# Batched float32 A·Bᵀ on one core: fourteen of sixteen stores move to GpSimd's DMA queue and start after the eighth load

## The chip, the cores and the metric

The kernel runs on one core of one Trainium2 chip. The metric is the device time in microseconds (us) of one execution. The kernel before took 127.14 us in the median of nine runs (126.47 to 127.92). The profile is one further execution, which took 126.65 us.

## The reference

```python
batch, m, k, n = 16, 512, 512, 512
a = np.random.randn(batch, m, k).astype(np.float32)
b = np.random.randn(batch, n, k).astype(np.float32)
out = np.matmul(a, b.transpose(0, 2, 1)).astype(np.float32)
```

There are sixteen independent 512x512x512 products. Both operands have the contraction dimension k last, so both have to be transposed before TensorE can multiply them. The inputs are 2 x 16.8 MB, the output is 16.8 MB, and each byte crosses once: 33.55 MB read and 16.78 MB written.

## The kernel before, in words

**Units.** Two batch elements form a pair, and there are eight pairs. A load fetches one operand of one pair: 2 MB, each of the 128 partitions taking 16 KB that are contiguous in memory. Loads are numbered 0 to 15; even ones are `a`, odd ones are `b`. The first two are issued as two halves of 1 MB each. A store writes one batch element: 1 MB, 8 KB per partition. Stores are numbered 0 to 15, and output k is what store k writes. `ld` has seven load slots and `ob` has seven output slots.

**Compute.** VectorE casts a load to bf16 in four instructions (lines 167 to 175), into the left and right halves of k. TensorE transposes 128x128 blocks against an identity (line 247) into PSUM tile `tp`. ScalarE copies A's transposes to `ta` (line 206), VectorE copies B's to `tb` (line 187). TensorE multiplies (line 266) into `ps`, and ScalarE copies `ps` to `ob` (line 224). Each of these engines runs a loop over the pairs and is held by semaphores alone.

**Semaphores that matter here.** `s_go` tells VectorE that half a load is there (two counts for a load). `s_cd` counts the first cast of each load; a load into a used slot waits for it. `s_out` counts finished outputs; a store waits for it. `s_of` counts free output slots; ScalarE takes counts from it before it writes outputs. It starts at seven.

**Order of the DMA work.** The string `ORDER`, written by hand, holds 16 letters L (load) and 15 letters S (store). SyncE (SP in the profile) walks it in the first loop (lines 92 to 118): for an L it waits for `s_cd` where the slot was used, then issues the load; for an S it waits for `s_out`, then issues the store. Since SP is one instruction stream, a letter waits for all letters before it. The DMA engines work through what SP issues in that order. The string begins with seven loads, has four more loads between the first two S, and ends with nine S.

GpSimd (POOL in the profile) walks the same string in the second loop (lines 123 to 145). For an L it waits until the load has landed and passes that on as `s_go`. For an S it waits until an old store has landed and passes that on as `s_of`. Store 0 alone is issued by GpSimd (line 135), after the fourth load has landed and output 0 is finished. ScalarE takes two counts of `s_of` at the head of each pair.

At the end SP waits for the last seven stores (lines 119, 120 and 279).

Of the kernel before, what the change touches and what calls it, by code (L numbers as in the profile page):

```python
# [10 lines left out]
def kernel(  # L11
# [6 lines left out]
    nc = tc.nc  # L18
    P = 128
    batch, M, K = a.shape  # L20
    _, N, _ = b.shape
    J = M // P
# [3 lines left out]
    pairs = batch // 2  # L26
    f32 = mybir.dt.float32
    bf16 = mybir.dt.bfloat16
    NL = 7
    NO = 7  # L30


    ORDER = "LLLLLLLSLLLLSLSSLSLSLLSSSSSSSSS"

    def sbuf(name, shape, dtype):
        return ctx.enter_context(nc.sbuf_tensor(name, shape, dtype))

    def sem(name):
        return tc.alloc_semaphore(name)

    with tc.tile_critical(no_gpsimd_drain=True):  # L41
        ident = sbuf("ident", [P, P], bf16)
        one = sbuf("one", [P, 1], f32)
        ld = sbuf("ld", [P, NL, 2 * J, K], f32)
# [5 lines left out]
        ob = sbuf("ob", [P, NO, J, N], f32)  # L50
# [3 lines left out]
        s_set = sem("s_set")  # L54
        s_ld = [sem(f"s_ld{i}") for i in range(NL)]
        s_second = [sem(f"s_second{i}") for i in range(2)]
        s_first = sem("s_first")
        s_st = [sem(f"s_st{i}") for i in range(NO)]

        def landed(n):  # L60
            return 16 * (n // NO + (n % NO > 0))


        s_go = sem("s_go")
        s_of = sem("s_of")
        s_cd = sem("s_cd")
# [11 lines left out]
        s_out = sem("s_out")  # L78
# [5 lines left out]
            out=ident[:], in_=ident[:], compare_op=mybir.AluOpType.not_equal, fill=1.0,  # L84
# [4 lines left out]

        n_ld, n_st = 0, 1
        for what in ORDER:
            if what == "L":
                u, slot = n_ld // 2, n_ld % NL
                src = (a if n_ld % 2 == 0 else b)[2 * u:2 * u + 2].rearrange(
                    "e (p j) k -> (e p) j k", j=2 * J
                )
                if n_ld >= NL:

                    nc.sync.wait_ge(s_cd, n_ld - NL + 2)
                if n_ld < 2:
                    nc.sync.dma_start(
                        ld[:, slot, :J, :], src[:, :J, :]
                    ).then_inc(s_ld[slot], 16)
                    nc.sync.dma_start(
                        ld[:, slot, J:, :], src[:, J:, :]
                    ).then_inc(s_second[slot], 16)
                else:
                    nc.sync.dma_start(ld[:, slot], src).then_inc(s_ld[slot], 16)  # L110
                n_ld += 1
            else:
                slot = n_st % NO
                nc.sync.wait_ge(s_out, n_st + 1)
                nc.sync.dma_start(
                    out[n_st].rearrange("(p j) n -> p j n", j=J), ob[:, slot]
                ).then_inc(s_st[slot], 16)
                n_st += 1
        for n in range(batch - NO, batch - 1):
            nc.sync.wait_ge(s_st[n % NO], landed(n))  # L120


        n_ld, n_st = 0, 1
        for what in ORDER:
            if what == "L":
                got = nc.gpsimd.wait_ge(s_ld[n_ld % NL], 16 * (n_ld // NL + 1))
                if n_ld < 2:
                    got.then_inc(s_go, 1)
                    nc.gpsimd.wait_ge(s_second[n_ld], 16).then_inc(s_go, 1)
                else:  # L130
                    got.then_inc(s_go, 2)
                n_ld += 1
                if n_ld == 4:
                    nc.gpsimd.wait_ge(s_out, 1)
                    nc.gpsimd.dma_start(  # L135
                        out[0].rearrange("(p j) n -> p j n", j=J), ob[:, 0]
                    ).then_inc(s_first, 16)
                elif n_ld == NL:
                    nc.gpsimd.wait_ge(s_first, 16).then_inc(s_of, 1)
            else:  # L140
                if n_st < batch - NO:
                    nc.gpsimd.wait_ge(
                        s_st[n_st % NO], landed(n_st)
                    ).then_inc(s_of, 1)
                n_st += 1

        def taker(engine):
            return lambda s, n: engine.wait_ge(s, n).then_inc(s, -n)  # L148
# [5 lines left out]
        take = taker(nc.vector)  # L154
# [3 lines left out]
        with nc.Fori(0, pairs, engines=[dve]) as u:  # L158
            for x, (h, w, s_c, s_w) in enumerate(
                ((ha, wa, s_ca, s_wa), (hb, wb, s_cb, s_wb))  # L160
            ):
                src = ld[:, bass.ds((u * 2 + x) % NL, 1)].rearrange("p o j k -> p (o j) k")
                take(s_go, 1)
                if x == 0:
# [3 lines left out]
                    out=h[:, :J, :], in_=src[:, :J, :HK]  # L168
# [4 lines left out]
                    out=h[:, J:, :], in_=src[:, J:, :HK]  # L173
                ).then_inc(s_c, 1)
                nc.vector.tensor_copy(  # L175
                    out=w[:, J:, :], in_=src[:, J:, HK:]
                ).then_inc(s_w, 1)
            for ko in range(KO):
# [5 lines left out]
                if ko == 1:  # L184
# [3 lines left out]
                    out=tb[:, ko, :],  # L188
# [5 lines left out]
        take = taker(nc.scalar)  # L194
# [3 lines left out]
        with nc.Fori(0, pairs, engines=[act]) as u:  # L198
            for ko in range(KO):

                if ko < KO - 1:
                    nc.scalar.wait_ge(s_ta, ko + 1)
                else:
                    take(s_ta, KO)
                for e in range(2):
                    c = nc.scalar.copy(  # L206
                        out=ta[:, ko, e * J * P:(e + 1) * J * P].rearrange(
                            "k (j p h) -> k j p h", j=J, h=2
                        ),
                        in_=tp[:, ko % 2, :, e * HP:(e + 1) * HP].rearrange(  # L210
                            "k (h j) p -> k j p h", h=2
                        ),
                    )
                c.then_inc(s_ea, 1)
            take(s_of, 2)
            for e in range(2):
                dst = ob[:, bass.ds((u * 2 + e) % NO, 1)].rearrange("m o j n -> m (o j) n")
                for j in range(J):
                    if j < J - 1:
                        nc.scalar.wait_ge(s_mm, j + 1)  # L220
                    else:
                        take(s_mm, J)

                    c = nc.scalar.copy(  # L224
                        out=dst[:, j, :].rearrange("m (p j) -> m p j", j=2 * J),
                        in_=ps[:, j, :].rearrange("m (j p) -> m p j", j=2 * J),
                    )
                    if e == 0:
                        c.then_inc(s_pv, 1)
                    elif j in (0, J - 1):  # L230

                        c.then_inc(s_out, 1)
# [3 lines left out]
        take = taker(nc.tensor)  # L236
# [40 lines left out]


    with tc.tile_critical(no_gpsimd_drain=True):
        nc.sync.wait_ge(s_st[(batch - 1) % NO], landed(batch - 1))  # L280


# [28 lines left out]
```

## Time and profile before

| what | value |
|---|---|
| median of nine runs | 127.14 us |
| range of the nine | 126.47 to 127.92 us |
| profiled execution | 126.65 us |
| its span, first to last instruction | 124.8 us |
| TensorE matmul busy | 93.2 us (75%) |
| VectorE busy | 70.5 us (56%) |
| ScalarE busy | 68.3 us (55%) |
| GpSimd busy | 1.4 us (1%) |
| bytes moved | 50.33 MB, mean 403 GB/s over the span |
| packet time, SP's queue q1 | 94.2% of sixteen engines' span |
| packet time, GpSimd's queue q0 | 2.0% |

The profiled execution is 1.85 us longer than its span (126.65 less 124.8) and 0.49 us shorter than the median. In the page's second part the span is cut into 40 slices of 3.12 us each: a digit is the busy share in tenths, the DMA row is the mean over the core's sixteen DMA engines, and the last row is what they moved in GB/s. The third part has a line for each DMA queue. In a line of waits or of a timeline, SPq, DVEq and PEq are the instruction sequencers of SyncE, VectorE and TensorE, and L115 is line 115 of the kernel.

The trace also has a record for each DMA packet, with queue, start, duration and size. A packet carries one partition's row: 16 KB for a load of 2 MB, 8 KB for a store or a half load. It does not say which of the sixteen DMA engines carried it. Times taken from these records are counted from the start of the span, as all others.

### The profile page before, as it was taken

The numbers are of one execution on the slowest core, as the hardware profiler recorded it, in microseconds if no ns is written. First come the engines' busy times: TensorE is split into PE (matmuls) and PEld (weight loads), VectorE is DVE, ScalarE is ACT, GpSimd is POOL, SyncE is SP. The second block draws the span as 40 slices with busy tenths as digits, with TensorE's granted clock in tenths as the row PEclk, the third lists the DMA queues.
The fourth block names the chain that finished last, engine by engine and source line by source line (L and its number), as shares of the span: only waits on it lengthen the run. The fifth ranks groups of instructions, "written<-read, shape, count | busy, mean of one in ns | idle before, by whom it ended". The sixth has DMA issues, their size and how long they took to land. (4 is left out here: it accounts for less than half of the span.)

```text
span 124.8 us, 2407 instructions
## 1 busy us (share of the span) xinstructions
PE 93.2 (75%) x768; PEld 58.4 (47%) x768; DVE 70.5 (56%) x112; ACT 68.3 (55%) x130; POOL 1.4 (1%) x7
## 2 busy tenths in 40 slices
PE   0005299998999999899989998994069999899000
PEld 0005295467347644754674476442069447734000
DVE  0056677748965873988579398161395956810000
ACT  4004234589468855966695589469006358945300
POOL 2000000020000000000000000000000000000000
PEclk9999999999999999999999999999955899999955
DMA  2999999999999999999999999999999999999970
GB/s 71 402 433 430 444 420 441 425 436 383 396 425 420 438 430 436 425 425 420 417 438 415 404 451 388 407 444 415 441 436 425 423 420 425 428 423 423 433 331 39
DMA packets 4896, 50.33 MB, mean 403 GB/s; under 512 B 544, under 2 KB 544, under 8 KB 544
## 3 DMA queue, kind: packets, MB, share of 16 engines
q1 hardware_dynamic: 4752, 49.29, 94.2%
q0 software_dynamic: 144, 1.05, 2.0%
HBM read 33.55 MB, written 16.78 MB: 403 GB/s over the span
## 5 line engine op out<-in xcount | busy, mean ns | idle before, releaser
L266 PE MATMUL ps<-tb,ta 128*128 128x512 bf16 x256 | 58.0, 380 | 0.4
L224 ACT COPY ob<-ps 128x512 f32 x64 | 34.7, 588 | 26.7 <-PE ps L266 26.7
L206 ACT COPY ta<-tp 128x512 bf16<-128x512 bf16 x64 | 32.9, 604 | 20.5 <-PE tp L247 20.5
L266 PEld LDWEIGHTS ps<-tb,ta 128*128 128x128 bf16 x256 | 24.4, 98 | 30.6 <-issue 4.0
L247 PE MATMUL tp<-ident,ha 128*128 128x128 bf16 x256 | 20.3, 236 | 12.8 <-PEq L148 12.8
L247 PE MATMUL tp<-ident,hb 128*128 128x128 bf16 x256 | 19.7, 238 | 9.4 <-PEq L148 9.2
L247 PEld LDWEIGHTS tp<-ident,ha 128*128 128x128 bf16 x256 | 17.4, 106 | 16.2 <-issue 14.7
L187 DVE COPY tb<-tp 128x1024 bf16<-128x1024 bf16 x32 | 21.4, 686 | 5.4 <-DVEq L148 5.3
L247 PEld LDWEIGHTS tp<-ident,hb 128*128 128x128 bf16 x256 | 17.5, 108 | 10.1 <-issue 10.1
L167 DVE CAST hb<-ld 128x1024 bf16 x8 | 5.6, 694 | 14.2 <-DVEq L148 14.2
L167 DVE CAST ha<-ld 128x1024 bf16 x8 | 5.5, 690 | 10.6 <-DVEq L148 10.6
L182 DVE COPY ha<-wa 128x2048 bf16<-128x2048 bf16 x8 | 5.6, 694 | 6.3 <-DVEq L148 6.0
L172 DVE CAST hb<-ld 128x1024 bf16 x8 | 5.5, 687 | 1.1 <-DVEq L148 1.1
L172 DVE CAST ha<-ld 128x1024 bf16 x8 | 5.5, 688 | 1.0 <-DVEq L148 1.0
L186 DVE COPY hb<-wb 128x2048 bf16<-128x2048 bf16 x8 | 5.5, 686 | 0.5 <-DVEq L148 0.5
L175 DVE CAST wa<-ld 128x1024 bf16 x8 | 5.5, 687 | 0.0
L170 DVE CAST wa<-ld 128x1024 bf16 x8 | 5.5, 686 | 0.0
L175 DVE CAST wb<-ld 128x1024 bf16 x8 | 5.5, 686 | 0.0
L170 DVE CAST wb<-ld 128x1024 bf16 x8 | 5.5, 686 | 0.0
L197 ACT ACT_TABLE_LOAD x1 | 1.3, 1283 | 1.1 <-SPq L41 1.1
L135 POOL DMA_DIRECT2D out_dram<-ob x1 | 0.7, 693 | 24.1 <-ACT ob L224 24.1
L83 POOL TENSOR_SCALAR_AFFINE_SELECT ident<-ident 128x128 bf16<-128x128 bf16 x1 | 0.3, 283 | 0.2 <-POOL ident L81 0.2
(6 smaller groups left out, 0.8 us busy)
## 6 DMA issues: line engine op xcount, KB each, us to landing
out_dram<-ob SPq DMA_DIRECT2D x15, 1024.0 KB, 28.2
ld<-in_a_dram SPq DMA_DIRECT2D x7, 2048.0 KB, 30.1
ld<-in_b_dram SPq DMA_DIRECT2D x7, 2048.0 KB, 30.6
ld<-in_a_dram SPq DMA_DIRECT2D x2, 1024.0 KB, 6.3
ld<-in_b_dram SPq DMA_DIRECT2D x2, 1024.0 KB, 10.4
out_dram<-ob POOLq DMA_DIRECT2D x1, 1024.0 KB, 13.0
```

The lines of the kernel that those rows point to most:

```text
L167: nc.vector.tensor_copy(out=h[:, :J, :], in_=src[:, :J, :HK]).then_inc(s_cd, 1)
L170: nc.vector.tensor_copy(out=w[:, :J, :], in_=src[:, :J, HK:])
L172: nc.vector.tensor_copy(out=h[:, J:, :], in_=src[:, J:, :HK]).then_inc(s_c, 1)
L175: nc.vector.tensor_copy(out=w[:, J:, :], in_=src[:, J:, HK:]).then_inc(s_w, 1)
L182: nc.vector.tensor_copy(out=ha[:], in_=wa[:]).then_inc(s_ca, 1)
L186: nc.vector.tensor_copy(out=hb[:], in_=wb[:]).then_inc(s_cb, 1)
L187: nc.vector.tensor_copy(out=tb[:, ko, :], in_=tp[:, 2 + ko % 2].rearrange("k j p -> k (j p)"),).then_inc(s_eb, 1)
L197: nc.scalar.copy(out=one[:], in_=nc.const_aps.tensor(1.0, (P, 1), f32))
L206: c = nc.scalar.copy(out=ta[:, ko, e * J * P:(e + 1) * J * P].rearrange("k (j p h) -> k j p h", j=J, h=2), in_=tp[:, ko % 2, :, e * HP:(e ...
L224: c = nc.scalar.copy(out=dst[:, j, :].rearrange("m (p j) -> m p j", j=2 * J), in_=ps[:, j, :].rearrange("m (j p) -> m p j", j=2 * J),)
L247: t = nc.tensor.transpose(tp[:, 2 * x + g, j, :], h[:, j, g * P:(g + 1) * P], ident[:])
L266: t = nc.tensor.matmul(ps[:, j, :], ta[:, ko, (e * J + j) * P:(e * J + j + 1) * P], tb[:, ko, :].rearrange("k (j p) -> k j p", j=2 * J)[:, ...
```

## The change

- `ORDER` is gone. SP issues loads only, and at the end stores 14 and 15. It issues the first seven loads, and then walks the loads: it waits until load n has landed, passes on `s_go`, and (for n from 1 to 9) issues load n+6, which waits on `s_cd` as before.
- GpSimd issues stores 0 to 13, in the order of a new string `STORES`: an S waits for `s_out` and issues a store, an O waits until the next old store has landed and passes on `s_of`. Ahead of the first it waits for `s_ld[0]` at 32, that is until load 7, the eighth, has landed.
- GpSimd no longer passes on `s_go`.
- Stores 14 and 15 have semaphores of their own (`s_last`), and the waits at the end follow.
- ScalarE takes one count of `s_of` for each output, not two for each pair.

```diff
-    ORDER = "LLLLLLLSLLLLSLSSLSLSLLSSSSSSSSS"
+    STORES = "SSSSOSOSOSSOSOSOSOSOSOS"
+    LAST = 2
...
-        s_first = sem("s_first")
+        s_last = [sem(f"s_last{i}") for i in range(LAST)]
...
+        def load(n):
+            u, slot = n // 2, n % NL
...
+            if n >= NL:
+
+                nc.sync.wait_ge(s_cd, n - NL + 2)
+            if n < 2:
...
             else:
+                nc.sync.dma_start(ld[:, slot], src).then_inc(s_ld[slot], 16)
+
+        for n in range(NL):
+            load(n)
+        for n in range(2 * pairs):
+            got = nc.sync.wait_ge(s_ld[n % NL], 16 * (n // NL + 1))
+            if n < 2:
+                got.then_inc(s_go, 1)
+                nc.sync.wait_ge(s_second[n], 16).then_inc(s_go, 1)
+            else:
+                got.then_inc(s_go, 2)
+
+            if n > 0 and n + NL - 1 < 2 * pairs:
+                load(n + NL - 1)
+
+        for n in range(batch - LAST, batch):
+            nc.sync.wait_ge(s_out, n + 1)
+            nc.sync.dma_start(
+                out[n].rearrange("(p j) n -> p j n", j=J), ob[:, n % NO]
+            ).then_inc(s_last[n % LAST], 16)
+        for n in range(batch - NO, batch - LAST):
+            nc.sync.wait_ge(s_st[n % NO], 16 * (n // NO + 1))
+        for n in range(batch - LAST, batch - 1):
+            nc.sync.wait_ge(s_last[n % LAST], 16)
+
+
+        n_st = n_of = 0
+        nc.gpsimd.wait_ge(s_ld[0], 32)
+        for what in STORES:
+            if what == "S":
                 slot = n_st % NO
-                nc.sync.wait_ge(s_out, n_st + 1)
-                nc.sync.dma_start(
+                nc.gpsimd.wait_ge(s_out, n_st + 1)
+                nc.gpsimd.dma_start(
                     out[n_st].rearrange("(p j) n -> p j n", j=J), ob[:, slot]
                 ).then_inc(s_st[slot], 16)
                 n_st += 1
...
             else:
-                if n_st < batch - NO:
-                    nc.gpsimd.wait_ge(
-                        s_st[n_st % NO], landed(n_st)
-                    ).then_inc(s_of, 1)
-                n_st += 1
+                nc.gpsimd.wait_ge(s_st[n_of % NO], 16 * (n_of // NO + 1)).then_inc(s_of, 1)
+                n_of += 1
...
-            take(s_of, 2)
             for e in range(2):
+                take(s_of, 1)
...
-        nc.sync.wait_ge(s_st[(batch - 1) % NO], landed(batch - 1))
+        nc.sync.wait_ge(s_last[(batch - 1) % LAST], 16)
```

More of the change, by code (lines that the diff above doesn't have):

```diff
@@ L56 @@
         s_second = [sem(f"s_second{i}") for i in range(2)]
-        s_first = sem("s_first")
+        s_last = [sem(f"s_last{i}") for i in range(LAST)]
         s_st = [sem(f"s_st{i}") for i in range(NO)]
-        def landed(n):
-            return 16 * (n // NO + (n % NO > 0))
         s_go = sem("s_go")
@@ L86 @@
         ).then_inc(s_set, 1)
[L92 to L102, printed above, removed]
-                    nc.sync.dma_start(
[L104 to L111, printed above, removed]
-            else:
+        def load(n):
+            u, slot = n // 2, n % NL
+            src = (a if n % 2 == 0 else b)[2 * u:2 * u + 2].rearrange(
+                "e (p j) k -> (e p) j k", j=2 * J
+            )
+            if n >= NL:
+                nc.sync.wait_ge(s_cd, n - NL + 2)
+            if n < 2:
+                nc.sync.dma_start(
+                    ld[:, slot, :J, :], src[:, :J, :]
+                ).then_inc(s_ld[slot], 16)
+                nc.sync.dma_start(
+                    ld[:, slot, J:, :], src[:, J:, :]
+                ).then_inc(s_second[slot], 16)
+            else:
+                nc.sync.dma_start(ld[:, slot], src).then_inc(s_ld[slot], 16)
@@ new lines @@
+        for n in range(NL):
[11 more added lines that the diff above has]
+            nc.sync.wait_ge(s_out, n + 1)
+            nc.sync.dma_start(
+                out[n].rearrange("(p j) n -> p j n", j=J), ob[:, n % NO]
+            ).then_inc(s_last[n % LAST], 16)
@@ L113 @@
+        for n in range(batch - NO, batch - LAST):
[6 more added lines that the diff above has]
+            if what == "S":
                 slot = n_st % NO
-                nc.sync.wait_ge(s_out, n_st + 1)
-                nc.sync.dma_start(
+                nc.gpsimd.wait_ge(s_out, n_st + 1)
+                nc.gpsimd.dma_start(
@@ L118 @@
                 n_st += 1
[L119 to L139, printed above, removed]
-            else:
-                if n_st < batch - NO:
-                    nc.gpsimd.wait_ge(
-                        s_st[n_st % NO], landed(n_st)
-                    ).then_inc(s_of, 1)
-                n_st += 1
+            else:
+                nc.gpsimd.wait_ge(s_st[n_of % NO], 16 * (n_of // NO + 1)).then_inc(s_of, 1)
+                n_of += 1
         def taker(engine):
```

## The prediction

> **What bounds the kernel now.** I read the page's second and third parts first: are the DMA engines ever idle, and who feeds them?
>
> ```profile
> DMA  2999999999999999999999999999999999999970
> GB/s 71 402 433 430 444 420 441 425 436 383 396 425 420 438 430 436 425 425 420 417 438 415 404 451 388 407 444 415 441 436 425 423 420 425 428 423 423 433 331 39
> ...
> q1 hardware_dynamic: 4752, 49.29, 94.2%
> q0 software_dynamic: 144, 1.05, 2.0%
> ```
>
> From slice 2 to slice 38 every slice shows nine tenths or more. The packets' time, 94.2% + 2.0%, is 120.1 us of 124.8. No compute engine is near that. So DMA sets the time, and the question is whether the sixteen engines stay full and at what rate. The busy table by stretches (columns: stretch, length, busy time of PE, PEld, DVE, ACT, POOL, clock, DMA share, GB/s) answers the second:
>
> ```profile
> 12.00:28.00 16.00, 12.97 (x104) 9.00 (x105) 11.10 (x19) 7.86 (x16) 0.69 (x1) 1.00 1.02 434
> 28.00:34.00 6.00, 5.45 (x57) 3.50 (x55) 5.50 (x10) 4.71 (x10) 0.00 (x0) 1.00 0.98 385
> 34.00:38.00 4.00, 4.00 (x21) 1.77 (x19) 3.01 (x6) 2.18 (x5) 0.00 (x0) 1.00 1.04 442
> 44.00:46.00 2.00, 2.00 (x10) 0.88 (x9) 2.00 (x4) 1.07 (x2) 0.00 (x0) 1.00 0.91 369
> 62.00:80.00 18.00, 16.90 (x166) 10.78 (x164) 12.47 (x20) 13.53 (x27) 0.00 (x0) 1.00 1.00 413
> 80.00:100.00 20.00, 13.89 (x100) 9.31 (x99) 11.14 (x18) 8.64 (x17) 0.00 (x0) 0.83 1.01 431
> 100.00:114.00 14.00, 13.45 (x109) 7.83 (x108) 6.71 (x11) 9.65 (x19) 0.00 (x0) 1.00 1.01 424
> ```
>
> Loads alone (12 to 28) run at 434, stores alone (100 to 114) at 424. There are dips at 28 to 34, at 44 and within 62 to 80. GpSimd's one store is in flight from 29.8 to 37.8 by the packet records; the first two thirds of that time show a dip and the last third none. Last, the timeline at the start of that store and at the end:
>
> ```profile
> 25.76 0.69 POOL L135 DMA_DIRECT2D out_dram<-ob  x1 [24.08 <-ACT ob L224]
> ...
> 101.78 0.69 DVE L167 CAST hb<-ld 128x1024 bf16 x1 [1.35 <-DVEq L148]
> ...
> 113.78 1.07 ACT L224 COPY ob<-ps 128x512 f32 x2 [0.69 <-PE ps L266]
> 114.39 2.51 SPq L115 DMA_DIRECT2D out_dram<-ob  x2
> 115.45 1.09 ACT L224 COPY ob<-ps 128x512 f32 x2 [0.60 <-PE ps L266]
> ```
>
> The last load's first cast starts at 101.78, and output 15 is complete at 115.45 + 1.09 = 116.54: 14.8 us from the last load to the last output. Store 15 is issued at 116.57. The last packet ends at 123.14, and the average engine is done near 121.2, since the engines finish between 120.5 and 123.1. So at 116.6 each still has four to six us of work.
>
> **What the Trainium skill says.** "DMA: Bandwidth & Descriptors", section "Issuing engines are not separate DMA queues": DMAs from SP and GpSimd run on the same 16 engines, and a second issuer saves only issue time. The trace agrees: with both queues active, 34 to 38 moved 442 GB/s, no more than loads and stores in one queue can show over four us. Same page, "Queues, rings and completion order": an engine takes turns between its queues, a packet at a time. The trace agrees: from 29.8 to 37.8 the packet records have 128 store packets beside 141 load packets, about one for one. "SBUF — State Buffer", section "SBUF: two separate sides", warns that GpSimd writes the descriptors of its DMAs and is locked out while VectorE runs in its two-port modes. The trace fits: that store was issued at 25.76 and its first packet came at 29.77, 4.0 us later, with VectorE busy for much of it; SP's first load took 1.0 us (0.95 to 1.97).
>
> **The change part by part.**
>
> *Hold-back.* Loads 0 to 7 are 16.8 MB. In the packet records a 16 KB packet takes 611 ns and an 8 KB one 309 ns, from SP and GpSimd alike. Data starts at 1.97; load 6 landed at 40.8 (the trace's semaphore records) behind 14.7 MB of loads and store 0 (2.5 us), so without that store it lands at 38.4, and load 7 4.9 us later, at about 43.4. Store 0's first packet, 4.0 us on, is at 47.5. Until then loads run alone. The SP queue stays full: load n+6 needs load n landed and cast, so from four to six loads of 4.9 us stand in line. Cost 0.
>
> *Sharing.* At 47.5 some 14.9 MB of loads are left, 57 packets an engine. One for one with store packets, a turn of both takes 0.611 + 0.309 = 0.92 us, so loads get 285 GB/s and stores 142. The last load is through at 47.5 + 57 x 0.92 = 99.9 on the average engine and, with the 1.5 us by which the slowest trails, at 101.4. Now its cast starts at 101.78: **the same time**. By 99.9 some 7.1 stores are out; 8.9 are left, at 2.47 us each 22.0 us: all data is through at 121.9 by this sum, against the 121.2 that the same bytes took before. Moving bytes in time removes none, so I take the difference as the coarseness of the sum, and 0 for it.
>
> *Supply of stores.* GpSimd's 14 issues at 0.69 us are 9.7 us of an engine busy 1.4; behind each wait stand only its later stores and `s_of`. Before store 4 four stores are out, later five; while loads run each takes 7.4 us, so the queue is never dry. Alone after 100, five are 12 us of work against about 6 us from a landing to the next one's first packet (1.3 + 0.7 + 4.0). Cost 0; if each issue waited unhidden after 100, seven stores x 4 us would be 28 us in place of 17, which is 11 us late. I keep a small part of that for the range.
>
> *Output slots.* Store k lands at about 47.5 + 7.4(k+1) + 1. Output 11 needs store 4, at 85.5, and ScalarE was ready for it at 82.7: a wait of 2.8 us. Behind it in ScalarE's queue are its copies for pair 6; TensorE's next work there, the transposes of pair 6's b, began at 91.75 before, because of its load. Output 13 needs store 6, at 100.3, about 0.7 us late; pair 7's cast comes at 101.4. Both are covered by waits for loads, cost 0; without the cover 3.5 us. Counting slots singly rather than in twos only shortens such waits.
>
> *Signals passed by SP.* Each load that SP issues (0.33 to 1.49 us in the trace) now lies ahead of the next `s_go`, and so does its wait for `s_cd`, the first cast of load n. VectorE has three more casts of 0.69 us before it can use load n+1: 2.1 us cover about 0.5. Cost 0, bound 8 x 0.5 = 4 us on VectorE, which waits for loads anyway. GpSimd is freed of it; nobody gains.
>
> *The last two stores* stay with SP at 114.4 and 116.6. Store 15 needs about 1.2 us to start and 2.5 us of its own: 120.3 at the earliest. The slowest engine ends at 123.1 anyway, so its cover is 2.8 us. The final waits are as before: from the last packet at 123.14 to the span's end 1.7 us.
>
> *Dips.* Packets beyond 611 and 309 ns add 1.8 us per engine now. Neither their cause nor their number after the change is shown. From below: all vanish, and the engines end level: -1.8 and -1.9. From above: the shared stretch at 385 rather than 434 GB/s costs 22.3 MB/0.385 - 22.3 MB/0.434 = 57.9 - 51.4 = +6.5 us. Dips so far stand near places where loads and stores mix, and there will be more mixing; half of one dip (28 to 34) came before GpSimd's first packet. I take +0.2.
>
> *Sum*: 126.65 + 0 (bytes, supply, slots, signals, tail) + 0.2 = 126.85 for an execution like the profiled one; the median of the runs lies 0.49 above that execution, so **127.3 us**.
>
> **The rivals.**
>
> *Mixing costs rate (slower).* The place is 47 to 100, where every engine alternates load and store; the price is up to 6.5 us. For it: 28 to 34, and the skill's lock on descriptor writing. Against: 34 to 38 at 442, and store packets of 309 ns in both queues. It decides above 0.6 us, that is at about 430 GB/s instead of 434. At 0.45 to 1 of the price: 130 to 133.6; I put it at 130.5.
>
> *The tail is exposed (slower).* If the stores get more than half of the turns, or start 4 us earlier (+2 us for the last load), the last load slips. It decides once output 15 comes over 2.8 us late. At 5 us late: 127.1 + 2.2 = 129.3. Against: the turns counted above.
>
> *The dips go (faster).* The first eight loads run unmixed, and the engines may end more evenly. Half of 1.8 + 1.9: 127.1 - 1.8 = 125.3. Against: nothing in the page ties the dips to SP's order.
>
> *It does nothing at all*, engines being full either way, is my forecast itself.
>
> **How the numbers follow.** A measurement of this kernel can tell about 0.5% (0.64 us) from no change. Forecast 127.3, own range 126.0 to 128.6: chance 0.66 (0.12 faster, 0.36 within, 0.18 slower). Mixing 0.14, tail 0.05, dips gone 0.15. Faster 0.12 + 0.15 = 0.27; same 0.36; slower 0.18 + 0.14 + 0.05 = 0.37. For eight in ten I leave out the upper half of mixing (0.07), the lower half of dips gone (0.07) and a few hundredths at the ends of the others: 125.5 to 130.5.
>
> **What would show it.** Loads alone near 430 GB/s until about 47; then both queues, packets one for one; last cast near 101.8; output 15 near 116.5; DMA share full until 120. GpSimd's queue should hold 14 stores, 14.7 MB. Wrong if the DMA row shows a hole (supply or tail), if 47 to 100 moves under 420 GB/s (mixing), or if the last cast comes after 104.

## The result, and the profile after

| | kernel before | changed kernel |
|---|---|---|
| median | 127.03 us (31 runs) | 125.91 us (10 runs) |
| range | 126.30 to 127.92 | 125.71 to 126.25 |
| profiled execution | 126.65 | 126.27 |
| its span | 124.8 | 124.5 |

The ratio is 0.9912, with a 95% interval of 0.9888 to 0.9936: the change makes the kernel 0.9% faster, some 1.1 us. I had forecast 127.3 us, no difference. The time lies in my range of 125.5 to 130.5, but in its corner, which stood there for a rival: the case that I had called "the dips go", put at 125.3 us and given a chance of 0.15.

DMA rows and queues on the changed kernel's page:

```profile
DMA  4999999999999999999999999999999999999970
GB/s 82 384 434 434 440 427 437 432 427 427 421 421 437 442 421 395 434 421 445 403 437 432 424 450 398 440 448 416 448 398 445 413 429 427 424 421 427 429 298 11
...
q1 hardware_dynamic: 2880, 35.65, 68.0%
q0 software_dynamic: 2016, 14.68, 28.0%
```

The DMA engines are as full as before: no slice from the second to the 38th is under nine tenths. Fourteen stores, 14.68 MB, went through GpSimd's queue. The packets' time is 68.0% + 28.0% = 96.0% of 124.5 us, 119.5 us, against 120.1 before. Next the busy table of the changed kernel, over stretches shown of the kernel before (last three columns: clock, DMA share, GB/s):

```profile
28.00:34.00 6.00, 5.45 (x63) 3.75 (x61) 5.11 (x9) 4.70 (x11) 0.00 (x0) 1.00 1.01 429
46.00:48.00 2.00, 2.00 (x12) 0.88 (x10) 2.00 (x5) 1.09 (x2) 0.13 (x1) 1.00 0.96 369
62.00:80.00 18.00, 16.90 (x168) 10.89 (x166) 13.75 (x23) 13.53 (x28) 2.22 (x4) 1.00 1.00 427
80.00:100.00 20.00, 17.46 (x126) 10.71 (x125) 10.06 (x17) 9.89 (x21) 1.06 (x2) 0.91 1.00 427
100.00:114.00 14.00, 10.94 (x93) 6.24 (x90) 6.28 (x10) 9.66 (x19) 1.95 (x3) 1.00 1.01 425
```

28 to 34 now moves 429 GB/s (385 before) and 62 to 80 moves 427 (413 before), though loads and stores are mixed through all of 48 to 98. One dip is left, at 46 to 48, when the first store starts. Mixing by itself costs nothing here.

The end shows best in the trace's semaphore records. Each transfer leaves sixteen counts there. I read one count as one of the sixteen DMA engines that is done with its share; it fits that the same number of counts stays late from transfer to transfer (seven of sixteen in each of the last fifteen transfers of the kernel before). These are the times of store 15's counts, in us, and after the earliest of them:

```
                     earliest at   8th     15th    last    engines over 0.8 us late
kernel before          120.77     +0.43   +2.66   +2.72    7
changed kernel         120.66     +0.15   +0.39   +2.44    1
```

The earliest DMA engine is done at nearly the same time in both. Before, seven engines came in over 0.8 us late; now fifteen are within 0.39 us and one trails.

The last count sets the time. In all eleven profiles of this document the execution took between 3.16 and 3.21 us more than the moment of its last count (126.65 and 123.49 before, 126.27 and 123.10 after).

### The profile page after: what moved, and what is told of

The parts are those of the page before. It is cut to its first block, busy times and chain, and to the rows that moved or that the text cites. A ratio compares the mean times of both kernels' runs of the same rounds, so it can differ in the third digit from the quotient of the medians.

```text
span 124.5 us, 2416 instructions
## 1 busy us (share of the span) xinstructions
PE 92.5 (74%) x768; PEld 58.0 (47%) x768; DVE 70.2 (56%) x112; ACT 68.0 (55%) x130; POOL 9.4 (8%) x20
## 3 DMA queue, kind: packets, MB, share of 16 engines
q0 software_dynamic: 2016, 14.68, 28.0%
## 5 line engine op out<-in xcount | busy, mean ns | idle before, releaser
L137 POOL DMA_DIRECT2D out_dram<-ob x14 | 8.8, 627 | 96.2 <-DMA out_dram<-ob 54.4
```

Of the source, the lines that this page charges most:

```text
L137: nc.gpsimd.dma_start(out[n_st].rearrange("(p j) n -> p j n", j=J), ob[:, slot]).then_inc(s_st[slot], 16)
```

## The experiments

**Theories.** *A*: on one queue that goes from stores to loads, load packets soon after the switch are slow, on some engines and not on others, and those engines stay late to the end; two queues taking turns never switch. *B*: the slow packets are the memory's own and fall anywhere. *C*: the gain is the order of the bytes, eight loads unmixed and then one load for each store, whichever queue. *D*: GpSimd's first DMA makes the burst at 28. *E*: the one engine that trails after the change is held back by GpSimd's queue.

**1. The kernel before, profiled again** (no edit).

> The kernel before, profiled once more, to see whether its slow load packets (bursts at 28 to 33, 44, 66 and 76 to 78 us) come back. Theory A (a queue that goes from stores to loads): they stand just after a store on SP's queue is followed by loads, so bursts are again at some of the places near 28, 44, 66, 76, 84 and 92 us, 1 to 2 us lost per engine in all, and never inside 12 to 27 or 47 to 61 us. Theory B (chance, the memory's own): bursts anywhere, 12 to 27 and 47 to 61 us too. Time 126.3 to 127.9 us either way.

It took 126.76 us. The busy table of this run:

```profile
28.00:34.00 6.00, 5.45 (x56) 3.44 (x54) 5.50 (x10) 4.66 (x10) 0.00 (x0) 1.00 1.01 389
44.00:46.00 2.00, 2.00 (x11) 0.89 (x10) 2.00 (x4) 1.07 (x2) 0.00 (x0) 1.00 1.00 352
66.00:68.00 2.00, 1.94 (x15) 0.88 (x13) 1.93 (x4) 0.77 (x2) 0.00 (x0) 1.00 1.05 418
76.00:78.00 2.00, 1.81 (x30) 1.55 (x28) 1.50 (x3) 2.00 (x5) 0.00 (x0) 1.00 0.97 385
```

The bursts are back at the same four places, with other sizes; by the packet records there is none at 84 or 92, and practically none elsewhere. Again seven engines are late at the end, the last by 2.81 us. B falls. In the packet records SP's stores run from 39.9 to 42.9, 61.8 to 65.0 and 69.1 to 75.8 us in the first profile of this kernel: the bursts at 44.4, 66.2 and 76.3 begin 0.5 to 1.5 us after each of these, and the loads' first packets behind these stores, some 2 us earlier, are of the usual length. Behind the two stores after these (to 84.0 and 91.3) there is no burst.

**2. One queue, in the order of the changed kernel.** Against the kernel before:

```diff
-    ORDER = "LLLLLLLSLLLLSLSSLSLSLLSSSSSSSSS"
+    ORDER = "LLLLLLLLL" + "SL" * 7 + "S" * 9
...
-            return 16 * (n // NO + (n % NO > 0))
+            return 16 * (n // NO + 1)
...
-        n_ld, n_st = 0, 1
+        n_ld, n_st = 0, 0
...
-                if n_ld == 4:
-                    nc.gpsimd.wait_ge(s_out, 1)
-                    nc.gpsimd.dma_start(
...
-            take(s_of, 2)
             for e in range(2):
+                take(s_of, 1)
```

> All sixteen stores on SP's queue, but in the byte order that the changed kernel has: nine loads, then store and load in turn seven times, then nine stores; a slot count for each output, as after the change. It parts the order from the second queue. Theory A (a queue that goes from stores to loads makes slow packets, two queues in turn don't): seven such changes, slow bursts after several of them, 1 to 2 us per engine, and a time like before, 126.5 to 127.5 us. Theory C (the gain is the order, eight loads unmixed and one load for each store): 125.7 to 126.3 us, as after the change.

Measured 126.77 us, ratio to before 0.9984 (0.9965 to 1.0003). At the end six engines are over 0.8 us late, the last by 2.73 us. The early part of its busy table:

```profile
28.00:34.00 6.00, 5.45 (x50) 3.22 (x48) 5.50 (x10) 4.19 (x9) 0.00 (x0) 1.00 1.01 431
44.00:47.00 3.00, 3.00 (x15) 1.37 (x14) 3.00 (x6) 2.09 (x4) 0.00 (x0) 1.00 0.99 366
```

The burst of 28 to 34 has moved with the first store, to 44 to 47. By the packet records two more follow, at 51 and 59, after SP's first two stores (47.1 to 50.1 and 54.5 to 58.3), and little after that. The order alone, with its slot counts taken singly, brings 0.16%, by the interval at most 0.35%, where the changed kernel gains 0.88%: C falls, and the second queue is what counts.

**3. No hold-back.** Against the changed kernel:

```diff
-        nc.gpsimd.wait_ge(s_ld[0], 32)
```

> The changed kernel without the hold-back: GpSimd's stores start as soon as output 0 is there (25.8 us). Loads get 285 GB/s from about 30 us, not from 47 us, so the last load is through about 6 us later, near 105 us, output 15 near 120 us, and the end is set by the tail: 127.5 to 128.5 us by my sum. Theory A says that no bursts of slow packets come in the mixed stretch, so that the loss is the tail alone. Theory C says bursts come back, and the DMA engines stay full to the end with a time near 127.

Measured 131.36 us, ratio 1.0331 (1.0295 to 1.0368). DMA rows of its page:

```profile
DMA  4999999999999999999999999999999999970193
GB/s 94 397 428 443 440 430 420 440 420 375 407 435 415 435 420 440 420 440 423 433 430 428 440 415 425 443 423 430 435 425 433 438 412 420 425 316 5 76 410 162
```

It is the tail: from slice 36 on the engines stand nearly idle (5.3 us without a store packet, 117.27 to 122.60), and then the last two stores come. There is a dip at the first store (slice 10, 375 GB/s) and, by the packet records, a small one near 39, and none in the 60 us of mixing after that. The direction and mechanism were right, the size was not: I said 127.5 to 128.5. I had put the last load near 105 us; its slowest engine landed it at 108.75. From its first cast (109.07) to output 15 (123.90) it took 14.8 us as in my sum, and store 15 needed 4.2 us from issue to landing (123.93 to 128.14), not 3.7.

**4. Store 0 on SP's queue.** Against the kernel before:

```diff
-    ORDER = "LLLLLLLSLLLLSLSSLSLSLLSSSSSSSSS"
+    ORDER = "LLLLLLLSSLLLLSLSSLSLSLLSSSSSSSSS"
...
-            return 16 * (n // NO + (n % NO > 0))
+            return 16 * (n // NO + 1)
...
-        n_ld, n_st = 0, 1
+        n_ld, n_st = 0, 0
...
-                if n_ld == 4:
-                    nc.gpsimd.wait_ge(s_out, 1)
-                    nc.gpsimd.dma_start(
```

> The kernel before with store 0 on SP's queue too, ahead of store 1; GpSimd issues no DMA. Theory D (GpSimd's first DMA brings the burst at 28 to 33 us, 0.47 us per engine, 2.3 us after its issue): that burst is gone, those near 44, 66 and 76 us stay; 126.5 to 127.0 us. If the burst is chance or belongs to the store on SP at 27.67 us, it stays and the time is 127.0.

Measured 127.38 us, ratio 1.0030 (1.0010 to 1.0049): slightly slower. Its busy table:

```profile
28.00:34.00 6.00, 5.45 (x56) 3.39 (x54) 5.50 (x10) 4.59 (x10) 0.00 (x0) 1.00 1.01 431
34.00:38.00 4.00, 4.00 (x20) 1.84 (x19) 2.92 (x5) 2.23 (x5) 0.00 (x0) 1.00 0.93 313
```

The burst at 28 is gone and a larger one stands at 34 to 38, just ahead of SP's first store packets at 37.7. D falls as stated: there is a burst around the first store of a run whichever queue carries it. Its cause stays open. It hits the engines about evenly (the spread of the next loads is no larger after it), so it shifts all of them; the later bursts spread them. At the end eight engines are over 0.8 us late, the last by 3.49 us; this profiled execution took 127.90 us, 0.5 us above the kernel's median.

**5. The changed kernel, profiled again** (no edit).

> The changed kernel, profiled once more. In its first profile 15 of 16 DMA engines finished store 15 within 0.39 us of each other and one 2.05 us after them; it fell back by about 0.15 us with each of GpSimd's stores. If that engine is a property of GpSimd's queue, one engine trails by 1.5 to 2.5 us again, and slow load packets are again only near 46 us (0.2 us per engine). If it was chance, another number of engines trails, or none. Time 125.7 to 126.3 us.

It took 125.98 us. Two engines are over 0.8 us late, one by 0.93 and one by 2.17 us. Slow load packets stand near 47 to 48 and, thinly, up to 60, some 0.4 us per engine in all, and none after that. One engine trailing the rest by over a us is part of this kernel.

**6. Hold-back of seven loads.** Against the changed kernel:

```diff
-        nc.gpsimd.wait_ge(s_ld[0], 32)
+        nc.gpsimd.wait_ge(s_ld[6], 16)
```

> The changed kernel with the stores held until the seventh load has landed (38.3 us), not the eighth (43.2 us). Stores take a third of the DMA from 4.9 us earlier on, so the last load is through 4.9/3 = 1.6 us later: output 15 at 114.7 + 1.6 = 116.3, its data at about 116.3 + 1.2 + 2.5 = 120.0 at the earliest, against 120.4 for the fifteen engines and 122.6 for the last. By my sum it is still covered: 125.9 to 126.3 us, no difference or 0.3 us slower. If the tail has less cover than I think, 127 us.

Measured 125.97 us, ratio 0.9926 (0.9901 to 0.9950): the eighth load makes no difference that can be seen. The busy table shows that it sits at the edge:

```profile
112.00:116.00 4.00, 4.00 (x21) 1.81 (x19) 0.00 (x0) 2.72 (x6) 0.00 (x0) 1.00 0.90 379
116.00:118.00 2.00, 1.19 (x6) 0.34 (x4) 0.00 (x0) 1.38 (x3) 0.00 (x0) 1.00 0.76 315
118.00:122.00 4.00, 0.00 (x0) 0.00 (x0) 0.00 (x0) 0.00 (x0) 0.00 (x0) 0.78 0.90 373
```

Output 15 comes at 117.98, not 116.3, and the DMA engines have a hole before it. In that hole the trailing engine catches up: store 15's counts come within 0.80 us, the last at 122.81 against 123.10 in the changed kernel's first profile. The tail now sets the end, at the same time.

**7. Six last stores from SP.** Against the changed kernel:

```diff
-    STORES = "SSSSOSOSOSSOSOSOSOSOSOS"
-    LAST = 2
+    STORES = "SSSSOSOSOSSOSOSOOOO"
+    LAST = 6
```

> The changed kernel with the last six stores on SP's queue, not the last two: GpSimd issues ten. Theory E (one DMA engine falls back by 0.15 us with each of GpSimd's stores and sets the end): it trails by 4 x 0.15 = 0.6 us less, and the time falls to about 125.3 us. Rival: that engine's lag is set by the mixed stretch before 98 us; then it is the same 1.3 to 2 us and the time 125.9 us. SP has no loads behind these stores, so theory A expects no slow packets from them.

Measured 125.80 us, ratio 0.9915 (0.9891 to 0.9940), as the changed kernel. One engine trails by 1.89 us, the 15th by 0.57. E expected 0.6 us less time, and 0.1 came; the rival fits better. But the engine trails by 0.3 to 0.55 us less than in the two profiles of the changed kernel (2.44 and 2.17), so this run alone doesn't settle it.

**8. The second queue is ScalarE's, not GpSimd's.** Against the changed kernel, GpSimd's loop and SP's two stores are left out, ScalarE issues all sixteen stores, its loop is unrolled, and:

```diff
+        def store(n):
+            nc.scalar.wait_ge(s_out, n + 1)
+            nc.scalar.dma_start(
+                out[n].rearrange("(p j) n -> p j n", j=J), ob[:, n % NO]
+            ).then_inc(s_st[n % NO], 16)
...
+            if u == 2:
+                nc.scalar.wait_ge(s_ld[0], 32)
+                for n in range(4):
+                    store(n)
             for e in range(2):
-                take(s_of, 1)
...
+                if n >= NO:
+                    nc.scalar.wait_ge(s_st[n % NO], 16 * (n // NO))
...
                         c.then_inc(s_out, 1)
+                        if u >= 2:
+                            store(n - 1 if j == 0 else n)
```

> The changed kernel with all stores on ScalarE's queue, which the chip's hardware serves as it does SP's: GpSimd issues nothing, ScalarE's loop is unrolled and issues each store behind the copies, the first four after load 7 has landed. It parts 'a second queue' from 'GpSimd's queue'. Theory A with E (two queues in turn keep the engines in step, GpSimd's descriptors hold one engine back): no bursts after 48 us, all sixteen engines done within 0.6 us, near 120.8, and 124.0 to 124.6 us. If the trailing engine has nothing to do with GpSimd, 125.9 us. If one issuing engine per queue doesn't matter and it is GpSimd that avoids the bursts, 126.8 us as with SP's single queue. ScalarE pays some 0.4 us for each issue, hidden while loads set the pace.

Measured 125.82 us, ratio 0.9922 (0.9896 to 0.9948). Its DMA queues:

```profile
q10 hardware_dynamic: 2304, 16.78, 32.1%
...
out_dram<-ob ACTq DMA_DIRECT2D x16, 1024.0 KB, 25.8
ld<-in_a_dram SPq DMA_DIRECT2D x7, 2048.0 KB, 30.6
```

The gain is the same with GpSimd out of the game: it belongs to the second queue, with either of two engines as its owner. There is a burst at 45 to 46, small slow packets at 61, and nothing after that. One engine trails here too, by 1.83 us (the 15th by 0.69). E falls: the trailing engine isn't GpSimd's doing.

**9. One queue with one switch back.** As experiment 2, with another order:

```diff
-    ORDER = "LLLLLLLLL" + "SL" * 7 + "S" * 9
+    ORDER = "L" * 12 + "S" * 7 + "L" * 4 + "S" * 9
```

> All stores on SP's single queue once more, but grouped: twelve loads, seven stores, four loads, nine stores. The queue goes from stores back to loads once (near 77 us), where the order of the changed kernel did so seven times and the kernel before four times. Theory A (each such change, until the engines are out of step, costs slow packets): one burst after the change back besides the one at the first stores, the last engine 1 to 1.5 us behind the first, 126.0 to 126.4 us. Rival: a single queue costs the same however often it changes, 126.8 us, the last engine 2.7 us behind. Output slots make ScalarE wait some us near 60; loads are ahead by then, so nothing of that reaches the end.

Measured 126.68 us, ratio 0.9992 (0.9976 to 1.0009): the rival's time. The busy table around the switch:

```profile
76.00:79.00 3.00, 3.00 (x15) 1.37 (x14) 1.90 (x4) 1.80 (x4) 0.00 (x0) 1.00 1.04 440
79.00:82.00 3.00, 2.70 (x42) 2.33 (x40) 1.51 (x3) 2.92 (x6) 0.00 (x0) 1.00 1.01 366
82.00:85.00 3.00, 2.75 (x32) 1.87 (x31) 2.27 (x4) 2.18 (x5) 0.00 (x0) 1.00 1.00 426
```

The seven stores end between 79.0 and 79.8 on the different engines. The first load packets behind them, from 78.8 on, take the usual 0.61 us; then, between 80.4 and 81.0, seven packets take 1.16 to 1.83 us (packet records). The counts of the load that follows, after their earliest: nine engines within 0.47 us, the other seven 0.9 to 1.7 us late. Before the switch all sixteen were within 0.92 us, fifteen within 0.58. This is the mechanism of A in the open. Its count was wrong: one switch costs about as much as seven, since the first one puts nearly half of the engines back by over a us. The rest of the lag comes later: the last count is 1.69 us behind the earliest at the last load and 2.70 at store 15, because one engine falls back further during the nine stores. That later switches find the engines out of step and therefore do little is an argument from these traces, not a test of its own.

## Why the prediction was wrong

**What held.** *Hold-back*: store 0's first packet came at 47.43 (I said 47.5), load 7 landed at 43.2 (43.4). *Sharing*: 48 to 98 moved 428 GB/s, packet for packet (872 of stores, 870 of loads); the last load landed between 98.3 and 100.6 (99.9 and 101.4). The timeline of the changed kernel has its first cast, ScalarE's wait for a slot, and the last outputs:

```profile
100.95 0.69 DVE L165 CAST hb<-ld 128x1024 bf16 x1 [4.83 <-DVEq L146]
...
85.17 2.06 ACT L222 COPY ob<-ps 128x512 f32 x4 [2.99 <-ACTq L146]
...
112.51 2.52 SPq L122 DMA_DIRECT2D out_dram<-ob  x2
113.57 1.09 ACT L222 COPY ob<-ps 128x512 f32 x2 [0.60 <-PE ps L264]
```

The cast starts at 100.95, against 101.78 before. *Output slots*: ScalarE waited 2.99 us for output 11's slot, until 85.17 (I said 2.8, until 85.5), and nothing came of it. *Supply*: no hole in the DMA row. *Tail*: output 15 at 114.66 rather than 116.5, so with more cover than I counted. The hold-back is what gives that cover: without it the tail costs 5.45 us (131.36 less 125.91). *Signals*: VectorE waited 21.5 us in all ahead of its casts, where it had waited 26.9. So none of the three signs that I had named as showing me wrong came up: all of them look at the mean of the engines or at the compute engines, none at how far apart the DMA engines end.

**What failed is the step on dips.** I saw 1.8 us of slow packets per engine and took the slowest engine to end 1.9 us behind the average (the sixteen counts give 1.7), wrote that "their cause" isn't shown, and took +0.2 because "there will be more mixing". I also wrote, of the rival, that "nothing in the page ties the dips to SP's order". The page doesn't; the packet records that I had used for durations do: each burst after 40 us stands just behind a store on SP's queue. Mixing was the wrong name for it. In one queue, all engines go from stores to loads within a us or so (at 79 in experiment 9), and nearly half of them lose about a us or more there. With two queues they alternate for 50 us, with slow packets that come to 0.1 and 0.3 us per engine (the two profiles, 48 to 98) and no packet over 0.85 us. Of the rival "the dips go" one reason fails, the unmixed first loads (experiment 2), and the other came true: the engines end more evenly.

Two readings of the Trainium skill in the prediction fail with it. I had taken from "DMA: Bandwidth & Descriptors", section "Issuing engines are not separate DMA queues", that a second issuer saves only issue time. Issue time was not what was short, and the second queue still gained 0.9% (experiments 2 and 8). And I had read the 4.0 us before GpSimd's first packet as the lock on descriptor writing of "SBUF — State Buffer", section "SBUF: two separate sides". ScalarE's queue took 3.6 us to its first packet (42.87 to 46.44, experiment 8) and SP's 3.4 us (99.83 to 103.27, experiment 7), both with the engines full, against 0.85 us for SP on idle engines (121.75 to 122.60, experiment 3). So most of that delay is not GpSimd's own.

The size: counting packets over their usual time by more than 10 ns, the excess fell from 1.8 and 1.9 us per engine in the two profiles of before to 1.1 and 1.2 in those of after. What counts is the last engine, not the average. In the single-queue kernels (before, experiments 2, 4 and 9) six to eight engines are over 0.8 us late at the end; in the two-queue kernels, GpSimd's or ScalarE's, one or two, and none where a hole in the DMA row precedes the last stores (experiments 3 and 6). Store 15 landed at 123.49 and 123.60 before, at 123.10 and 122.81 after, 0.6 us earlier in the mean. The other kernels agree: 123.49 and 123.51 in experiments 2 and 9, 124.74 in experiment 4, which was slower; 122.81, 122.55 and 122.57 in experiments 6, 7 and 8.

The medians differ by 1.1. The other 0.5 us isn't shown, since executions without a profile have no such records. It probably is lateness too. Both profiled executions of before, 126.65 and 126.76, lie under its median of 127.03, and its times spread over 1.6 us (31 runs), those of the changed kernel over 0.5 (10 runs). The one profile of a slower single-queue execution, in experiment 4, has its last count 3.49 us behind the earliest. My forecast also carried the 0.49 us between one profiled execution and the median over to the changed kernel, whose profiled execution turned out 0.36 us above its median.

**What stays open.** Why packets some 2 us after a switch are slow and why only on some engines; whether it takes one queue for that, or only that all engines switch at once, which no experiment here parts; the burst around the first store of a run; and the one engine that trails by 1.8 to 2.4 us with two queues. It falls back while stores run, in some single-queue kernels as well; it does so without any store on GpSimd's queue too (experiment 8). Whether the profiler has a part in it wasn't tried. No version beat the changed kernel: with six stores on SP or all on ScalarE it takes 125.80 and 125.82 us, within the spread of its own runs.

## What to carry to other kernels

Here the last of the sixteen DMA engines set the end, to a few hundredths of a us, while every mean over the engines looked full. In a kernel that DMA bounds, look at how far apart a late transfer's sixteen counts land, and trace the gaps back to where they opened. A queue that goes from stores back to loads opened such a gap here, and giving the stores a queue of their own closed it; which engine owned that queue made no difference. The two queues shared by turns, so pick the moment when the second one starts, since stores that start early take their third of the bandwidth from the loads on which the tail depends.

## What the runs showed of the hardware

- On one queue that went from stores back to loads, the first load packets of 16 KB took the usual 0.61 us; some 2 us on, packets took up to 1.83 us, on about half of the engines, once per run or in a few steps. In 50 us of two queues taking turns (48 to 98) no load packet took over 0.85 us in the changed kernel's two profiles.
- A second queue of GpSimd and one of ScalarE gave the same time, 125.91 and 125.82 us. GpSimd's first packet came 3.9 us after its issue (43.49 to 47.43), as in the kernel before (4.0); a queue of ScalarE's or SP's that started while the engines were full took 3.6 and 3.4 us, SP's on idle engines 0.85.
- In eleven profiles the execution ended 3.16 to 3.21 us after the last of the sixteen counts of the last store.
- Around the first store of a run, load packets are slow by 0.2 to 0.8 us per engine in all, beginning some us ahead of its first data packet: at 28.4 for 29.8 (GpSimd), at 34 for 37.7 (SP), at 46.2 for 47.4 (GpSimd, changed kernel).
